# Conditioned hybrid layer on one core: the up-projection's half-size products for nine pairs of tiles in place of seven, and the MLP gate's first half computed earlier

## The chip, the core and the metric

The kernel runs on one core of a Trainium2 chip. Five engines work side by side, each through its own list of instructions: TensorE (PE, with its weight loads PEld), VectorE (DVE), ScalarE (ACT), GpSimd (POOL) and SyncE (SP), which here only issues DMAs. ACT and POOL issue DMAs too. They wait for one another on semaphores. The metric is the device time of one execution in microseconds, lower being better; all inputs and the output are fp32 in HBM.

## The reference

One decoder layer on 512 tokens with 1,024 channels: an attention part and a gated MLP, both conditioned by a vector c through `w_ada`. Only the second part and the end of the first matter here:

```python
mod = cs @ w_ada[l] + b_ada[l]
sh1, sc1, gt1, sh2, sc2, gt2 = [m[:, None, :] for m in jnp.split(mod, 6, axis=-1)]
...
mix = jnp.concatenate([o_hg, o_nsa], axis=-1) @ w_out[l]
x = x + gt1 * mix

h2 = rmsnorm(x, norm2_g[l]) * (1.0 + sc2) + sh2
u = causal_dwconv(h2 @ w_up[l], conv_w[l], conv_b[l])
a, v = jnp.split(u, 2, axis=-1)
x = x + gt2 * ((jax.nn.silu(a) * v) @ w_down[l])
```

`w_up` is 1024 x 5632 (two halves of D_FF = 2816, that is 22 tiles of 128 columns each), `w_down` 2816 x 1024. `gt2`, "the gate" in this document, is one row of 1,024 numbers, spread over all partitions.

## The kernel before

**Products.** Each fp32 operand is split into a rounded high part and the rest (`split`: ACT copies the high part, DVE subtracts), and each product is three matmuls (`mm3`, lines 156 to 158): high x high, high x low, low x high. All tiles of weights pass through this.

**Output projection** (lines 1577 to 1608 and the loop at 1948). Four token tiles i of 128 tokens. `hg_mix` normalises a tile's HGRN2 heads (an ACT square, a DVE sum, the power of `rstd` on POOL, a DVE multiply `on`), `hg_flip` transposes and splits it, `out_mm` multiplies, `out_sum` adds the residual and lets ACT sum the squares, `out_norm` turns them into the reciprocal root (DVE, then POOL's power), `out_scale` makes `hx`, and `h2_flip`, `h2_scale` and `h2_split` transpose it on TensorE, apply the conditioning and split it into `h2T`, the up-projection's right side. In the loop TensorE's list has `out_mm(i)` followed by `h2_flip(i - 1)`.

**Up-projection.** Stage st = 2f + s is tile f (0 to 21) of half s. A plain stage is `up_mm`: 8 blocks of 128 channels x 3 matmuls with 512 columns. `up_post` is the convolution (one ACT step, two DVE steps), then SiLU for s = 0 or the product with the other half for s = 1, after which `g_parts` lists the splits that the down-projection needs; the `x` tokens take them off the list one by one.

Tiles come in pairs: pair or unit j holds f = 2j and 2j + 1. In a unit, tile 2j (stages 4j and 4j + 1) is done by seven products P1 to P7 of half-size (Strassen's scheme over channel halves and token halves; `sprod`, four blocks x 3 matmuls with 256 columns), and tile 2j + 1 by two plain stages, called B and C. The product scheme needs sums of the weight quarters and of h2 (`hS`, eight granules of memory) and extra splits on ACT and DVE. The order within a unit is written out in `UNIT` (line 48); a token with a prime prepares the next unit. `PRO` (line 47) orders stages 0 to 7, `g` takes a step of the gate, `q` runs `up_post`. `NU = 8` is the last unit; the loop of line 1988 runs units 2 to 8, seven pairs. After it, the eight stages 36 to 43 run plain (lines 1993 to 2007, ordered by `PLAIN`, two of them with a low half made by a DMA that accumulates on POOL's queue).

**Memory.** `G` hands out one of 33 granules of 4 KB per partition. Each pair leaves two granules for the down-projection, `gP[j]` and `gQ[j]`, and parks others in HBM. `AWAY = (0, 1)` names the pairs whose `gQ` is parked too (`park`, DMA on ACT's queue) and read back in the first down phase (`load_away`, on SP's).

**The gate** (`ada_last`, line 1399). For each half of 512 columns: eight weight tiles from HBM, multiplied and added into an accumulator by DVE (lines 1410, 1415, 1420), a split, two matmuls with a matrix of ones (1426, 1427), an ACT copy. It is a generator: each `next(ada2)` does a step. The first half is stepped in `PRO` and in units 2 to 8, the second in the plain stages, all DMAs on SP's queue.

**Down-projection.** Again seven products, in three phases (`phase`) and a tail; `forms` prepares its weights, three forms ahead (`look`, `ready`), in buffers `whi`/`wlo` (two) and `aw` (one).

SP's, ACT's and POOL's DMA queues are worked off in program order, so a DMA that waits for its buffer holds up those behind it.

Of the kernel before, what the change touches and what calls it, by code (L numbers as in the profile page):

```python
# [20 lines left out]
P = 128  # L21
# [19 lines left out]
NB = 2  # L41
NU = 8
AWAY = (0, 1)
CUT = {"B": 6, "C": 7}
ADD = (1, 1)
PLAIN = "2 A1 1 1 A2 1 1 1"
PRO = ("t t g x M1 M2 t t t t F3 M3 F4 t A5 q0 M4 q1 q2 F6 q3 M5 M6 A7 x q4 g x q5 x t x n1' ns' f2' nc' n5' q6 na' g s4' m0' x x M7 m1' x f6' f7' x x x x f4'")
UNIT = ("P1 S P5 w n1' ns' x f3 B0 P6 P2 B1 V x f2' nc' n5' h1 x p-1 f4' P7 x m0' P3 h0' W p2 g p0 na' C0 P4 x x x C1 s4' p1 x m1' x f6' x x x f7'")
# [63 lines left out]
def hybrid_layer_kernel(ctx: ExitStack, tc: tile.TileContext, d: dict, out: bass.AP, dbg=None):  # L112
# [133 lines left out]

    made = [0]

    def form(src, added=False):

        made[0] += 1
        if made[0] % 3 != 2:
            hi = wp.tile(list(src.shape), F32R, tag="whi", name=nm("whi"))
            lo = wp.tile(list(src.shape), F32R, tag="wlo", name=nm("wlo"))
        else:
            t = wp.tile([P, 2] + list(src.shape)[1:], F32R, tag="aw", name=nm("w3"), bufs=1)
            hi, lo = t[:, 0], t[:, 1]
# [1019 lines left out]

    def hg_mix(i):
        ps = PS("hgo")
# [11 lines left out]
        r = SM([P, 8], "hrs")  # L1291
        rstd(r[:, 0:4], s[:, 0:4], 1.0 / P, 4.0 * EPS)
        on = TMP([P, 4, P], tag="on")
        ve.tensor_tensor(on, ps.rearrange("p (h e) -> p h e", h=4),
                         r[:, 0:4].unsqueeze(2).to_broadcast([P, 4, P]), ALU.mult)
        ons[i] = on

    def hg_flip(i):
        on = ons.pop(i)
        ps = PS()  # L1300
        for h in range(4):
            pe.transpose(ps[:, h * P:(h + 1) * P], on[:, h], ident)
        m = G([2, 4, P], F32R, s="mixH")
        t = TMP([P, 4, P], tag="og")
        for pr in range(2):
            ve.scalar_tensor_tensor(t[:, 2 * pr:2 * pr + 2], ps[:, pr * 256:pr * 256 + 256]
                                    .rearrange("p (h t) -> p h t", h=2), hgg,
                                    HGT[pr][:, :, i * P:(i + 1) * P], ALU.mult, ALU.mult)
        split(m[:, 0], m[:, 1], t)
        mixH[i] = m  # L1310
# [88 lines left out]
    def ada_last(s, res):  # L1399
        for q in range(2):  # L1400
            acc = res[:, q * 512:(q + 1) * 512]
            c0 = s * D + q * 512
            gp.memset(acc, 0.0)
            sp.dma_start(acc[0:1], d["b_ada"][:, c0:c0 + 512])
            for k in range(KT if q else 0):
                raw = TMP([P, 512], tag="ada2r")
                sp.dma_start(raw, ada_view[:, k, c0:c0 + 512])
                if k:
                    yield
                    ve.scalar_tensor_tensor(acc, last, cs[:, k - 1:k], acc, ALU.mult, ALU.add)  # L1410
                last = raw
            for k in range(0 if q else KT):
                last = res[:, 512:]
                if k:
                    ve.scalar_tensor_tensor(acc, last, cs[:, k - 1:k], acc, ALU.mult, ALU.add)
                sp.dma_start(last, ada_view[:, k, c0:c0 + 512])
                if k < KT - 1:
                    yield
            yield
# [6 lines left out]
            pe.matmul(ps, onesr, hi, start=True, stop=False)
# [150 lines left out]
    for i in range(NT):  # L1577
        x1.append(G([D], s="x1"))
        sp.dma_start(x1[i], x_view[:, i])
    next(gate1)  # L1580
    hg_mix(0)
    next(gate1)
    hg_mix(1)
    out_mm(0, 0, KN)
    cols_sum(acol)
    hg_flip(0)
    hg_mix(2)
    hg_mix(3)
    out_mm(1, 0, KN)
# [4 lines left out]
    hg_flip(1)  # L1594
    hg_flip(2)
    out_mm(3, 0, KN)
# [19 lines left out]
    def up_mm(st, sl, ks=range(KT)):  # L1616
        if st not in us:
            us[st] = PS("u")
            if st not in wts:
                wts[st] = next_parts(st < nst - 2, added=st >= 4 * NU + 4 and PLAIN.split()[st - 4 * NU - 4][0] == "A")  # L1620
        hi, lo = wts[st]
# [113 lines left out]
    def do(j, tok):  # L1735
        last = j == NU
        if tok.endswith("'"):
            if last:
                if tok in ("n1'", "m0'"):
                    piece()  # L1740
                return
            return do_(j + 1, tok[:-1])
        return do_(j, tok)

    def do_(j, tok):
        lo_, hi_ = lo_half, hi_half
# [71 lines left out]
    def g_parts(f, y):  # L1818
# [3 lines left out]
        if not odd:  # L1822
# [18 lines left out]
                     (split, st34[:, 0], st34[:, 1], s34),  # L1841
                     (lambda: None,),
                     (park, j, st22, st34)])

    def park(j, st22, st34):
        if j in AWAY:
            sc.dma_start(pk26[:, AWAY.index(j)], f32(gQ.pop(j)))
        sc.dma_start(pk22[:, j], f32(st22))
        sc.dma_start(pk34[:, j], f32(st34))
# [79 lines left out]

    def look():  # L1930
        w = next(source, False)
        if w is None:
            w = next(source)
        if w is not False:
            ready.append(w)

    def dn_out(acc, i, half, c0=0, c1=512):
# [5 lines left out]

    gt2 = wp.tile([P, D], F32, tag="xin", name="gt2", bufs=1)
    ada2 = ada_last(5, gt2)
    lo_half, hi_half, full = slice(0, 256), slice(256, 512), slice(0, 512)
    nst = 2 * NFF
    for i in range(NT):
# [24 lines left out]
    for tok in PRO.split():  # L1973
# [7 lines left out]
        elif tok[0] == "q":  # L1981
            up_post(int(tok[1]))
        elif tok[0] in "txg":
            do_(1, tok)
# [6 lines left out]
    assert not tw  # L1991
    first = 4 * NU + 4
    for st in range(first, nst):
        up_mm(st, full)
        if st >= nst - 2:
            look()
        if st == first:
            up_post(st - 1)
        elif st > first + 1:
            up_post(st - 2)  # L2000
        for _ in range(int(PLAIN.split()[st - first][-1])):
            next(ada2, None)

    look()
    up_post(nst - 2, False)
    bR, bW, bS, bV = ([PS("dn") for _ in range(2)] for _ in range(4))
# [101 lines left out]
```

## Time and profile before

| what | value |
|---|---|
| median of 3 runs (lowest to highest) | 675.23 us (674.49 to 675.26) |
| the profiled execution: its own time, its span | 674.35 us, 672.6 us |
| output projection's token loop | about 302 to 333 us |
| stages 0 to 7 | about 327 to 372 us |
| units 2 to 8 | 372.3 to 520.2 us |
| plain stages 36 to 43 | 520.2 to 563.8 us |
| down-projection | 564.2 us to the end |
| HBM traffic | 105.01 MB read, 13.90 MB written |

The span goes from the first to the last instruction of the program. In rows of the order of time, the first number is the start from the span's start, the second the duration, then engine, source line, operation, what is written and read, the shape, and in brackets the idle time of the engine before it and what ended it. Durations of matmuls overlap, so their price is read from the distance of their starts. A row of the waits gives the total, the number of waits and the longest.

### The profile page before, as it was taken

Reading aid. Unit: us, or ns where it says so; the run is one execution under the profiler, and the core shown is the slowest. Engines: PE = TensorE matmul, PEld = TensorE weight load, DVE = VectorE, ACT = ScalarE, POOL = GpSimd, SP = SyncE. Lnnn points to the kernel's source line nnn. Section 1 sums busy time; section 2 is a strip of 40 time slices with the busy share of each in tenths; the row PEclk is TensorE's granted clock in tenths of the full one; section 3 lists DMA queues with packets and bytes.
Section 4 is the critical chain, followed back from the end, with each engine's and each line's share of the span. In section 5 each row is a group of like instructions: output and inputs, shape, how many; then the busy total and the mean of one; then the engine's idle time right before and its main releaser. Section 6 shows DMA issues by size and latency. Waiting matters only on the chain.

```text
span 672.6 us, 10869 instructions
## 1 busy us (share of the span) xinstructions
PE 664.9 (99%) x3999; PEld 565.1 (84%) x3999; DVE 577.8 (86%) x1155; ACT 392.6 (58%) x757; POOL 60.0 (9%) x80
## 2 busy tenths in 40 slices
PE   8999999999999999999999999999999999999998
PEld 4678898788898889888998888989888888888886
DVE  5688988999998997687878988998898789988787
ACT  5564446666677688335665766667675455553431
POOL 1006144200000000200000011010110000000000
PEclk9999999999999999999999999999999999999999
DMA  9998444388042132435436677986779773979932
GB/s 279 287 322 269 145 157 138 106 288 254 11 147 95 33 107 99 172 96 161 140 95 172 179 196 198 242 218 175 187 181 277 217 234 124 393 259 398 388 112 94
DMA packets 110473, 128.52 MB, mean 191 GB/s; under 512 B 7067, under 2 KB 84691, under 8 KB 110421
## 3 DMA queue, kind: packets, MB, share of 16 engines
q1 hardware_dynamic: 103541, 106.89, 51.1%
q0 software_dynamic: 2448, 8.91, 6.9%
q10 hardware_dynamic: 4432, 12.04, 4.7%
q8 instruction: 31, 0.51, 0.3%
q14 instruction: 21, 0.17, 0.1%
HBM read 105.01 MB, written 13.90 MB: 177 GB/s over the span
## 4 chain that ended last, share of the span: by engine, by line
PE 92%; SPq 3%; DMA 2%; DVE 1%; issue 0%; ACTq 0%; ACT 0%
PE u L156 11%; PE u L158 11%; PE u L157 11%; PE dn L157 5%; PE dn L156 5%; PE dn L158 5%; PE pT L156 3%; PE pT L158 3%; PE pT L157 3%; PE F L1059 3%; PE oT L1087 3%; PE oh L158 2%; PE oh L156 2%; PE oh L157 2%; SPq L317 2%; PE lev L1188 2%
## 5 line engine op out<-in xcount | busy, mean ns | idle before, releaser
L156 PE MATMUL u<-h2h,whi 128*128 128x512 f32 (+1 forms) x208 | 78.0, 375 | 0.0
L157 PE MATMUL u<-h2l,whi 128*128 128x512 f32 (+1 forms) x208 | 77.8, 374 | 0.0
L158 PE MATMUL u<-h2h,wlo 128*128 128x512 f32 (+1 forms) x208 | 77.6, 373 | 0.0
L153 DVE TENSOR_TENSOR wlo<-raw,whi 128x1024 fp32r<-128x1024 f32 (+1 forms) x38 | 44.5, 1170 | 6.7 <-ACT whi L152 6.5
L152 ACT CAST whi<-raw 128x1024 fp32r<-128x1024 f32 (+1 forms) x38 | 38.3, 1008 | 18.8 <-PE u L157 7.3
L158 PEld LDWEIGHTS u<-h2h,wlo 128*128 128x128 f32 x208 | 39.2, 188 | 7.5 <-DVE wlo L153 0.4
L156 PEld LDWEIGHTS u<-h2h,whi 128*128 128x128 f32 x208 | 39.3, 189 | 6.0
L157 PEld LDWEIGHTS u<-h2l,whi 128*128 128x128 f32 x208 | 39.3, 189 | 5.8
L1027 ACT ACTIVATE pt<-pt,mx 128x128 f32<-128x128 f32 (+3 forms) x64 | 35.9, 562 | 11.8 <-DVE mx L1011 10.7
L1634 DVE SCALAR_TENSOR_TENSOR y<-u,cv,y 128x511 f32<-128x511 f32 x44 | 32.8, 745 | 11.4 <-ACT y L1633 11.4
L156 PE MATMUL pT<-hT,whi 128*128 128x512 f32 x96 | 39.2, 408 | 0.0
L1638 ACT ACTIVATE y<-y 128x512 f32<-128x512 f32 x21 | 13.3, 633 | 42.0 <-DVE y L1635 42.0
L158 PE MATMUL pT<-hT,wlo 128*128 128x512 f32 x96 | 37.7, 393 | 0.0
L157 PE MATMUL pT<-hT,whi 128*128 128x512 f32 x96 | 37.6, 391 | 0.0
L1011 DVE CUSTOM_DVE_ANT_0 pt<-S,cmask 128x128 f32<-128x128 f32 (+3 forms) x64 | 29.7, 484 | 6.5 <-PE S L1006 6.3
L1066 ACT COPY pT<-F 128x512 f32<-128x512 f32 (+2 forms) x52 | 25.9, 503 | 14.4 <-PE F L1059 11.2
L1635 DVE SCALAR_TENSOR_TENSOR y<-u,cv,y 128x510 f32<-128x510 f32 x44 | 32.9, 749 | 1.6
L1633 ACT ACTIVATE y<-u,cv 128x512 f32<-128x512 f32 x44 | 33.8, 771 | 0.0
L393 POOL TENSOR_TENSOR hrs<-hrs,mhalf 128x4 f32<-128x4 f32 (+2 forms) x16 | 20.0, 1259 | 136.4 <-DVE hrs L392 136.3
L157 PE MATMUL u<-h2l,w 128*128 128x256 f32 (+1 forms) x84 | 28.0, 333 | 0.0
L156 PE MATMUL u<-h2h,w 128*128 128x256 f32 (+1 forms) x84 | 28.0, 333 | 0.0
L158 PE MATMUL u<-h2h,w 128*128 128x256 f32 (+1 forms) x84 | 28.0, 333 | 0.0
(456 smaller groups left out, 2079.2 us busy)
## 6 DMA issues: line engine op xcount, KB each, us to landing
raw<-in_w_up SPq DMA_DIRECT2D x44, 512.0 KB, 5.6
aw<-in_w_ada SPq DMA_DIRECT2D x24, 512.0 KB, 3.6
raw<-in_w_down SPq DMA_DIRECT2D x10, 1024.0 KB
ada<-in_w_ada SPq DMA_DIRECT2D x32, 256.0 KB, 5.8
wlo<-raw POOLq DMA_DIRECT2D x15, 512.0 KB, 4.6
raw<-in_w_in SPq DMA_DIRECT2D x7, 1024.0 KB, 6.1
rawd<-in_w_down SPq DMA_DIRECT2D x12, 512.0 KB, 10.3
pk<-st ACTq DMA_DIRECT2D x11, 512.0 KB, 4.0
```

What stands on the lines that cost most here:

```text
L152: sc.copy(hi, src)
L153: (eng or ve).tensor_tensor(lo, src, f32(hi), ALU.subtract)
L156: pe.matmul(o, ah, bh, start=start, stop=False, skip_group_check=True)
L157: pe.matmul(o, ah, bl, start=False, stop=False, skip_group_check=True)
L158: pe.matmul(o, al, bh, start=False, stop=stop, skip_group_check=True)
L1011: ve.tensor_tensor_reduce(pt[:, sl], ps[:, sl], cmask[:, 512 - W:512], -1.0, 1e30, ALU.add, ALU.min, mx[:, e:e + 1])
L1027: sc.activation(pt[:, sl], pt[:, sl], AF.Exp, bias=mx[:, e:e + 1], scale=-1.0, accum_out=su[:, h % 2, e:e + 1])
L1059: pe.transpose(ps[:, j * P:(j + 1) * P], src[:, j * P:(j + 1) * P], ident)
L1066: sc.copy(pT, ps[:, 0:n * P])
L1633: sc.activation(y, u, AF.Identity, bias=cv[:, 132 + c:133 + c], scale=cv[:, 88 + c:89 + c])
L1634: ve.scalar_tensor_tensor(y[:, 1:], u[:, :T - 1], cv[:, 44 + c:45 + c], y[:, 1:], ALU.mult, ALU.add)
L1635: ve.scalar_tensor_tensor(y[:, 2:], u[:, :T - 2], cv[:, c:c + 1], y[:, 2:], ALU.mult, ALU.add)
```

## The change

`NU` becomes 10, so units 2 to 10, nine pairs, are done by half-size products and no stage after them is plain; `PLAIN` is empty and its loop is gone. `AWAY` grows to six pairs. In the last unit three tokens with a prime call `look` and so prepare the first three forms of the down-projection, the third of them in granules (`wide`). One more matmul of 256 columns stands behind the last unit's P1; it writes the half of its bank that P1 leaves out and that DVE overwrites later.

The gate's generator is cut into finer steps (40 in all, multiply and DMA apart). The first half runs during the output projection: its DMAs and bias go through POOL's queue, its multiplies stand between the steps of `hg_mix`, `hg_flip` and the token loop, and it is closed in `PRO` (split behind A5, matmuls ahead of stage 6, copy behind q5). The second half runs in `PRO`'s end and units 2 to 10, with its weights in a part of the constants that is no longer read, on SP's queue.

```diff
-NU = 8
-AWAY = (0, 1)
+NU = 10
+AWAY = (0, 1, 2, 3, 4, 5)
...
-PLAIN = "2 A1 1 1 A2 1 1 1"
-PRO = ("t t g x M1 M2 t t t t F3 M3 F4 t A5 q0 M4 q1 q2 F6 q3 M5 M6 A7 x q4 g x q5 x t x n1' ns' f2' nc' n5' q6 na' g s4' m0' x x M7 m1' x f6' f7' x x x x f4'")
+PLAIN = ""
+PRO = ("t t x M1 M2 t t t t F3 M3 F4 t A5 g q0 M4 q1 q2 F6 q3 M5 G M6 A7 x q4 x q5 G x t x n1' ns' f2' nc' n5' q6 na' s4' m0' x x M7 m1' g x f6' f7' x x x x f4'")
...
     def form(src, added=False):
-        made[0] += 1
-        if made[0] % 3 != 2:
+        made[0] += not wide[0]
+        if wide[0]:
+            hi, lo = (G(list(src.shape)[1:], F32R, s="wg") for _ in range(2))
+        elif made[0] % 3 != 2:
...
         rstd(r[:, 0:4], s[:, 0:4], 1.0 / P, 4.0 * EPS)
+        between()
         on = TMP([P, 4, P], tag="on")
...
-        split(m[:, 0], m[:, 1], t)
+        sc.copy(m[:, 0], t)
+        between()
+        ve.tensor_tensor(m[:, 1], t, f32(m[:, 0]), ALU.subtract)
...
     def ada_last(s, res):
         for q in range(2):
             acc = res[:, q * 512:(q + 1) * 512]
+            last = cb[:, C_LMASK:C_LMASK + 512] if q else res[:, 512:]
             c0 = s * D + q * 512
             gp.memset(acc, 0.0)
-            sp.dma_start(acc[0:1], d["b_ada"][:, c0:c0 + 512])
...
+            gp.dma_start(acc[0:1], d["b_ada"][:, c0:c0 + 512])
+            for k in range(KT):
                 if k:
                     ve.scalar_tensor_tensor(acc, last, cs[:, k - 1:k], acc, ALU.mult, ALU.add)
+                yield
+                (sp if q else gp).dma_start(last, ada_view[:, k, c0:c0 + 512])
+                yield
             ve.scalar_tensor_tensor(acc, last, cs[:, k:k + 1], acc, ALU.mult, ALU.add)
             hi = TMP([P, 512], F32R, tag="rhi")
             lo = TMP([P, 512], F32R, tag="rlo")
             split(hi, lo, acc)
             yield
+            yield
             ps = PS()
             pe.matmul(ps, onesr, hi, start=True, stop=False)
             pe.matmul(ps, onesr, lo, start=False, stop=True)
+            yield
             sc.copy(acc, ps)
             yield
+
+    def gate_step(n=2):
+        for _ in range(n):
+            next(ada2, None)
...
+    gt2 = wp.tile([P, D], F32, tag="xin", name="gt2", bufs=1)
+    ada2 = ada_last(5, gt2)
+    gate_step()
     next(gate1)
     hg_mix(0)
     next(gate1)
-    hg_mix(1)
+    hg_mix(1, partial(gate_step, 1))
+    gate_step(1)
     out_mm(0, 0, KN)
...
-    hg_mix(3)
+    hg_mix(3, partial(gate_step, 1))
+    gate_step(1)
...
-    hg_flip(2)
+    hg_flip(2, partial(gate_step, 1))
+    gate_step(1)
...
             if last:
-                if tok in ("n1'", "m0'"):
-                    piece()
+                if tok in ("nc'", "m0'", "na'"):
+                    look(tok == "na'")
                 return
...
             sprod(u(1, lo_), w[1], h2_quarter(0, lo_), True)
+            if last:
+                pe.matmul(u(1, hi_), w[1][0][:, 0], h2_quarter(0, lo_)[0][0], start=False, stop=False,
+                          skip_group_check=True)
...
-        elif tok == "g":
-            next(ada2, None)
+        elif tok in ("g", "G"):
+            gate_step(2 if tok == "g" else 1)
...
-                     (lambda: None,),
+                     (park_q, j),
                      (park, j, st22, st34)])
...
-    def park(j, st22, st34):
+    def park_q(j):
         if j in AWAY:
             sc.dma_start(pk26[:, AWAY.index(j)], f32(gQ.pop(j)))
...
         sc.dma_start(x1d[:, i], x1[i])
+        gate_step(1)
         out_norm(i)
+        gate_step(1)
...
-    first = 4 * NU + 4
-    for st in range(first, nst):
-        up_mm(st, full)
...
-    look()
-    up_post(nst - 2, False)
+    gate_step()
+    assert next(ada2, 0) == 0
...
         if k == 0:
-            sc.activation(ys[nst - 2], ys[nst - 2], AF.Silu)
+            pass
         elif k == 1:
             up_post(nst - 1)
         elif k % 2:
             step(3)
-            load_away(k // 2 - 1)
+            load_away(k - 3)
+            load_away(k - 2)
```

More of the change, by code (lines that the diff above doesn't have):

```diff
@@ L247, in hybrid_layer_kernel @@
     made = [0]
+    wide = [False]
     def form(src, added=False):
-        made[0] += 1
-        if made[0] % 3 != 2:
+        made[0] += not wide[0]
+        if wide[0]:
+            hi, lo = (G(list(src.shape)[1:], F32R, s="wg") for _ in range(2))
+        elif made[0] % 3 != 2:
             hi = wp.tile(list(src.shape), F32R, tag="whi", name=nm("whi"))
@@ L1276, in hybrid_layer_kernel, with hg_mix @@
     mixH = [None] * NT
-    def hg_mix(i):
+    def hg_mix(i, between=lambda: None):
         ps = PS("hgo")
@@ L1296, in hg_mix, with hg_flip @@
         ons[i] = on
-    def hg_flip(i):
+    def hg_flip(i, between=lambda: None):
         on = ons.pop(i)
@@ L1401, in ada_last @@
             acc = res[:, q * 512:(q + 1) * 512]
+            last = cb[:, C_LMASK:C_LMASK + 512] if q else res[:, 512:]
             c0 = s * D + q * 512
             gp.memset(acc, 0.0)
-            sp.dma_start(acc[0:1], d["b_ada"][:, c0:c0 + 512])
[L1405 to L1413, printed above, removed]
+            gp.dma_start(acc[0:1], d["b_ada"][:, c0:c0 + 512])
+            for k in range(KT):
                 if k:
                     ve.scalar_tensor_tensor(acc, last, cs[:, k - 1:k], acc, ALU.mult, ALU.add)
[L1416 to L1419, printed above, removed]
+                yield
+                (sp if q else gp).dma_start(last, ada_view[:, k, c0:c0 + 512])
+                yield
             ve.scalar_tensor_tensor(acc, last, cs[:, k:k + 1], acc, ALU.mult, ALU.add)
@@ L1619, in up_mm @@
             if st not in wts:
-                wts[st] = next_parts(st < nst - 2, added=st >= 4 * NU + 4 and PLAIN.split()[st - 4 * NU - 4][0] == "A")
+                wts[st] = next_parts(st < nst - 2, added=False)
         hi, lo = wts[st]
@@ L1745, in do_ @@
     def do_(j, tok):
+        last = j == NU
         lo_, hi_ = lo_half, hi_half
@@ L1841, in g_parts, with park @@
                      (split, st34[:, 0], st34[:, 1], s34),
-                     (lambda: None,),
+                     (park_q, j),
                      (park, j, st22, st34)])
-    def park(j, st22, st34):
+    def park_q(j):
         if j in AWAY:
             sc.dma_start(pk26[:, AWAY.index(j)], f32(gQ.pop(j)))
+    def park(j, st22, st34):
         sc.dma_start(pk22[:, j], f32(st22))
@@ L1928, in sums_first, with look @@
             raise AssertionError
-    def look():
+    def look(g=False):
+        wide[0] = g
         w = next(source, False)
@@ L1935, in look @@
             ready.append(w)
+        wide[0] = False
     def dn_out(acc, i, half, c0=0, c1=512):
@@ L1942, in dn_out @@
         sp.dma_start(out_view[:, i, cols], t)
-    gt2 = wp.tile([P, D], F32, tag="xin", name="gt2", bufs=1)
-    ada2 = ada_last(5, gt2)
     lo_half, hi_half, full = slice(0, 256), slice(256, 512), slice(0, 512)
@@ L1982, in hybrid_layer_kernel @@
             up_post(int(tok[1]))
-        elif tok[0] in "txg":
+        elif tok[0] in "txgG":
             do_(1, tok)
@@ L1991, in hybrid_layer_kernel @@
     assert not tw
-    first = 4 * NU + 4
-    for st in range(first, nst):
-        up_mm(st, full)
-        if st >= nst - 2:
-            look()
[L1997 to L2006, printed above, removed]
-    up_post(nst - 2, False)
+    gate_step()
+    assert next(ada2, 0) == 0
     bR, bW, bS, bV = ([PS("dn") for _ in range(2)] for _ in range(4))
```

## The prediction

> **What bounds the kernel now.** I read the page first, then the waits of the weight loads, then TensorE's order of time for the last pairs of tiles, then the same stretches for the other engines.
>
> ```profile
> span 672.6 us, 10869 instructions
> PE 664.9 (99%) x3999; PEld 565.1 (84%) x3999; DVE 577.8 (86%) x1155; ACT 392.6 (58%) x757; POOL 60.0 (9%) x80
> PE 92%; SPq 3%; DMA 2%; DVE 1%; issue 0%; ACTq 0%; ACT 0%
> PEld u L158 <- DVE wlo L153: 0.4, 1, 0.4
> PEld dn L157 <- DVE wlo L153: 0.3, 1, 0.3
> ```
>
> TensorE is 92% of the chain that ended last. The two PEld rows are all that weight loads waited for another engine from 300 us on. So every matmul issued less is time won, as long as the others keep pace; and whatever another engine delays beyond its slack is lost whole. The price of a product is the distance between starts, since durations overlap:
>
> ```profile
> 477.72 0.28 PE L156 MATMUL u<-h2h,w 128*128 128x256 f32 x1
> 477.84 0.28 PE L157 MATMUL u<-h2l,w 128*128 128x256 f32 x1
> ...
> 498.75 0.28 PE L156 MATMUL u<-h2h,w 128*128 128x256 f32 x1
> ...
> 520.23 0.40 PE L156 MATMUL u<-h2h,w 128*128 128x512 f32 x1
> ...
> 563.76 0.39 PE L1426 MATMUL ps<-rhi,onesr 128*128 128x512 f32 x1
> ...
> 564.21 0.39 PE L156 MATMUL dn<-whi,gP 128*128 128x512 f32 x1
> ```
>
> Half-size matmuls (256 columns) start 0.12 us apart. Unit 7 runs from 477.72 to 498.75, **21.03 us**. The eight plain stages run from 520.23 to 563.76, **43.53 us**, 5.44 each or 0.227 for each of 24 full matmuls (512 columns). Half a gate costs two matmuls, 0.45 us (563.76 to 564.21).
>
> **The change part by part.** *TensorE's sum.* The eight plain stages go and units 9 and 10 come, each seven half-size products and two full stages: 2 x 21.03 = 42.06. That is **-1.47 us**. The columns saved are those of six full matmuls a unit, which would be 1.4 us; but 84 half-size matmuls at 0.12 are 10.1 us, where the 48 full ones that they replace are 10.9, so a unit wins 0.8 or less. The extra matmul after P1 of the last unit has 256 columns: **+0.12**. The four gate matmuls change places only: the first half's go from unit 8 to a place ahead of stage 6, the second half's into unit 10. **0.**
>
> *Do units 9 and 10 hold unit 7's pace?* Unit 7 already carried what unit 9 will: the preparation of the next unit, the gate's last multiply and its split.
>
> ```profile
> 477.72:498.75 21.03, 21.03 (x134) 19.08 (x133) 18.93 (x35) 14.87 (x26) 1.75 (x2) 1.00 0.79 200
> 520.23:563.76 43.53, 43.53 (x194) 36.04 (x193) 36.41 (x58) 22.19 (x36) 1.75 (x2) 1.00 0.65 207
> 393.60:414.60 21.00, 21.00 (x133) 19.07 (x132) 18.60 (x35) 14.19 (x25) 1.73 (x2) 1.00 0.83 222
> 399.84 0.33 ACTq L1847 DMA_DIRECT2D pk<-gQ  x1
> ```
>
> The columns are PE, PEld, DVE, ACT, POOL, then clock and DMA share. DVE is busy 18.93 of 21.03 us, so about 2 us of each unit are left to it: tight, but TensorE leads. The four new parks (512 KB each, in units 3 to 6) are covered by unit 3, which parks one granule today (399.84) at a DMA share of 0.83 and shows 21.00 busy of 21.00. If that cover failed, ACT would be late by 0.33 us of issue a unit, of its 6 us of idle time. **0.**
>
> In the last unit the first three down weights replace the next unit's preparation:
>
> ```profile
> L153 DVE TENSOR_TENSOR wq<-raw,wq 128x512 fp32r<-128x512 f32 x35 | 23.9, 685 | 0.7 <-ACT wq L152 0.7
> 554.75 1.22 DVE L153 TENSOR_TENSOR wlo<-raw,whi 128x1024 fp32r<-128x1024 f32 x1
> 576.19 1.22 DVE L153 TENSOR_TENSOR wlo<-keep,whi 128x1024 fp32r<-128x1024 f32 x1
> ...
> 577.81 0.39 PE L156 MATMUL dn<-whi,gP 128*128 128x512 f32 x1
> ```
>
> Ten 512-column operations of 0.69 (6.9 us) leave DVE, five of 1,024 columns at 1.22 (two sums and three low halves, 6.1 us) come. The tightest form of the first down phase is ready at 577.41 (576.19 + 1.22), 0.4 us before its product at 577.81. Afterwards the third form is made before stage 43's matmuls, not after them, and stage 42's convolution too, so DVE enters the phase with less behind it. Bounds: 0.4 better than now to 0.4 of stall; I take **0**, from the DVE sum.
>
> *The first half of the gate moves* from units 2 to 8 into the output projection: seven multiplies on DVE, eight weight loads and the bias from SP's queue to POOL's. In the loop over the four token tiles each multiply stands where DVE waits today:
>
> ```profile
> 310.93 0.55 POOL L393 TENSOR_TENSOR rs<-rs,mhalf 128x1 f32<-128x1 f32 x1 [24.84 <-DVE rs L392]
> 311.51 0.89 DVE L1522 TENSOR_SCALAR hx<-x,rs 128x512 f32<-128x512 f32 x2 [0.66 <-POOL rs L393]
> 314.30 0.69 DVE L1510 TENSOR_TENSOR x<-x,tmp 128x512 f32<-128x512 f32 x1
> 315.78 0.16 DVE L1515 TENSOR_TENSOR ss<-ss 128x1 f32<-128x1 f32 x1 [0.79 <-ACT sq L1512]
> ...
> 331.33 0.87 DVE L1522 TENSOR_SCALAR hx<-x,rs 128x512 f32<-128x512 f32 x2
> ...
> 332.70 0.49 PE L1532 MATMUL ps<-cb,hx 128*128 128x128 f32 x3
> 332.86 0.87 PE ps L1532 x8
> ...
> 373.28 0.75 DVE L1415 SCALAR_TENSOR_TENSOR gt<-gt,cs 128x512 f32<-128x512 f32 x1
> 373.94 0.69 DVE L1685 TENSOR_TENSOR raw<-raw 128x512 f32<-128x512 f32 x1
> ```
>
> A multiply of 0.75 fits the gap of 0.79 (314.99 to 315.78), if its weights have landed. Its DMA is issued on POOL behind the rstd power, at 311.48 (310.93 + 0.55); the next multiply wants it at 314.99, **3.5 us** later. No row has this DMA; the nearest are these:
>
> ```profile
> gt<-in_w_ada SPq DMA_DIRECT2D x8, 256.0 KB, 2.8
> wlo<-raw POOLq DMA_DIRECT2D x15, 512.0 KB, 4.6
> rawd<-in_w_down SPq DMA_DIRECT2D x12, 512.0 KB, 10.3
> 502.48 0.87 POOL L1695 DMA_DIRECT2D wlo<-raw  x1 [9.16 <-ACT gP L152]
> DMA  9600000019910010000279799999950000796006
> ```
>
> The same bytes land in 2.8 us from SP; POOL's issue takes 0.87 of work, so I take 3.3 (nearest: same bytes, same source, half a microsecond for POOL). Ends: 2.8 and 10.3, the latter from a stage with full DMA engines. The last row is the DMA share from 311 to 333 us, 0.55 us a digit: the engines stand idle from 312 to 315, when the first of these transfers flies. Behind a waiting multiply on DVE stand ss, rstd, the scaling of h2 and of hx, the low halves and the next weight's subtraction; TensorE waits for hx. At the last transposes hx is complete at 332.20 (331.33 + 0.87), and its second half is wanted four transposes of 0.11 (0.87 for eight) after the start at 332.70: **0.9 us of slack**. At the taken 3.3 us the term is **0**; at 10.3 it is the slow rival below. The three multiplies before the loop stand in DVE's waits for POOL's power or for an ACT copy, and their weights were issued a whole step earlier: 0, and at worst the 0.1 by which a multiply overhangs its gap.
>
> *Stages 4 to 7.* The one stall, unit 2's first B matmul:
>
> ```profile
> 345.86 1.22 DVE L153 TENSOR_TENSOR hS<-hB,hS 128x1024 fp32r<-128x1024 f32 x1
> 347.20 0.77 ACT L1633 ACTIVATE y<-u,cv 128x512 f32<-128x512 f32 x1
> 374.55 1.22 DVE L153 TENSOR_TENSOR wlo<-raw,whi 128x1024 fp32r<-128x1024 f32 x1
> 375.42 0.40 PE L157 MATMUL u<-h2l,whi 128*128 128x512 f32 x1
> 375.82 0.50 PE L158 MATMUL u<-h2h,wlo 128*128 128x512 f32 x1
> ```
>
> The step there takes 0.40 where 0.23 is usual, and the next is long too: I put the loss at 0.26. The change takes the multiply at 373.28 away (-0.66, to the start of the next at 373.94) and puts a multiply, an ACT copy and a subtraction ahead of the first convolution. The multiply can start when DVE is through at 347.0 (345.86 + 1.22, overlapping a little) and ends at 347.7, the copy of 0.6 ends at 348.3, so the ACT step now at 347.20 slips by about 1.05. DVE then reaches this weight 0.39 late, while the two gate matmuls ahead of stage 6 move TensorE itself 0.45 on. The stall goes from 0.26 to about 0.2: **-0.08** at most, which I take. Ends: -0.26 (gone) and +0.4 (the slip counts whole). This is an estimate from these rows.
>
> **Sum:** -1.47 + 0.12 - 0.08 = **-1.43 us**. The profiled execution took 674.35 us, 1.75 around its span of 672.6; the median of the runs shown, 675.23, lies 0.88 above it. So the profiled execution would be 672.9 and the median **673.8 us**, or -0.21%. About 0.2% (1.35 us) is what a measurement of this kernel can tell from no change: the forecast sits on that line.
>
> **The rivals.** *Given back (chance 0.18):* the slip ahead of stage 4, or the entry to the down phase, costs 0.3 to 1.2 us, the term left at 0 there. For it: slack of 0.4 at 577.81 and DVE's chain in front of 374.55. Against: the DVE sum is lighter in the last unit. Time 674.1 to 675.0.
>
> *Slower (0.12):* the gate's DMAs on POOL land late in the token loop. With a landing of L, DVE is late by L - 3.5 in the second turn and by about L - 5.2 more in each of the next two (those turns are 7 us apart, 6.45 of wait and 0.54 of work on POOL, where the second follows the first by 5.3); TensorE loses that less 0.9. At L = 5.4 this is 1.4 and eats the gain; at 6.5 it is 4.7, time 678.5. Against it: the idle DMA engines in the row above and the 4.6 of twice the bytes; for it: 10.3 under load.
>
> ```profile
> 323.21 0.54 POOL L393 TENSOR_TENSOR rs<-rs,mhalf 128x1 f32<-128x1 f32 x1 [6.45 <-DVE rs L392]
> ```
>
> One mechanism would push it there without load: hx is scaled (0.89 for two, 0.45 each, where x's addition of as many elements takes 0.69) just where POOL issues the DMA; if POOL has to wait for it, L grows by up to 0.9. I give that case 0.04 of the 0.12. The Trainium skill ("SBUF — State Buffer", SBUF: two separate sides) says that DVE in its two-port mode locks POOL out and so holds up descriptors of DMAs from POOL's queue. No row here shows it. By that rule, and with the 4.6 of twice the bytes, L would be 5.5: DVE 2.6 late, TensorE 1.7, time 675.5.
>
> *It does not do what it says (0.04):* reloading six granules adds 2 MB in the first down phase, where
>
> ```profile
> 563.80:594.00 30.20, 30.20 (x135) 25.02 (x134) 27.72 (x37) 17.84 (x26) 0.00 (x0) 1.00 0.84 326
> ```
>
> DMA share is already 0.84 at 326 GB/s; 2.1 MB more at that rate is 6.4 us of backlog. If the next weights wait for it, TensorE loses 1 to 3 us: 675 to 677. Against it: the reloaded granules are wanted one phase later, from about 594 on.
>
> **How the numbers follow.** Forecast 0.66, split 0.42 faster to 0.24 same, since its own range is 673.2 to 674.4 around a line at 673.9. Given back 0.18, all same. Slower rival 0.12: 0.10 slower, 0.02 same. The last 0.04: half and half. Faster 0.42, same 0.46, slower 0.12. Range: down to 672.6 (the waits of both PEld rows gone, -1.35 - 0.26 - 0.3 = -1.9, and 0.7 for the runs' own spread, 674.49 to 675.23), up to 675.8 (1.2 given back, 675.0, and as much spread); the slow rival beyond it is left out.
>
> **What would show it.** Right: P1 of units 9 and 10 21.0 us apart, the last unit 21.6 with gate and extra matmul, the first dn matmul near 562.8, no DVE wait on a gate DMA in the token loop, no PEld wait beyond those two. Wrong: a TensorE wait on hx's transposes, on wlo ahead of unit 2, or on dn in the first products.

## The result: slower by 7 us, and the profile after

| | time, us | ratio to the kernel before, with its 95% interval |
|---|---|---|
| kernel before, 5 runs beside it | 675.23 (674.32 to 675.29) | |
| changed kernel, 5 runs | 682.31 (681.23 to 683.38) | 1.011 [1.0096, 1.0124] |
| forecast | 673.8 (672.6 to 675.8) | 0.998 |

The profiled execution of the changed kernel took 681.23 us around a span of 679.5. The page of the changed kernel, its first lines and the chain of work that ended last:

```profile
span 679.5 us, 11071 instructions
PE 666.9 (98%) x4072; PEld 567.0 (83%) x4072; DVE 586.2 (86%) x1175; ACT 399.7 (59%) x773; POOL 68.3 (10%) x92
PE 64%; DVE 17%; DMA 6%; ACT 5%; SPq 4%; issue 2%; ACTq 1%; DVEq 0%
```

TensorE's share of the chain fell from 92% to 64%, while its busy share of the span fell by one point only. A busy share does not show who sets the end. The waits of the weight loads from 300 us on do (total, number, longest), in the changed kernel:

```profile
PEld u L156 <- ACT u L1781: 6.3, 6, 1.3
PEld dn L157 <- DVE wlo L153: 3.0, 3, 1.8
PEld u L158 <- DVE wlo L153: 1.0, 1, 1.0
```

Before there were two such rows, of 0.4 and 0.3 us. The new first row is product P6, which waits six times for ACT's copy of token S (line 1781 now). The changed kernel by unit, from the view by stretches (same columns as in the prediction):

```profile
372.36:394.75 22.39, 21.62 (x133) 18.95 (x132) 19.42 (x34) 15.09 (x26) 2.80 (x4) 1.00 0.77 209
...
438.49:460.69 22.20, 21.30 (x134) 19.00 (x133) 19.40 (x35) 14.30 (x25) 1.72 (x2) 1.00 0.81 214
...
504.74:525.76 21.02, 21.02 (x133) 19.07 (x132) 19.17 (x35) 14.29 (x25) 1.75 (x2) 1.00 0.79 202
...
546.79:568.16 21.37, 21.37 (x135) 19.38 (x134) 17.71 (x30) 12.62 (x22) 0.88 (x1) 1.00 0.64 209
```

Units 2 to 7, the six in which a `gQ` is parked, take 21.8 to 22.4 us. Units 8 and 9 take 21.02 and 21.03, as forecast. The last window ends one matmul ahead of the down phase; to the phase's first product at 568.39 (below) the last unit takes 21.60, as forecast too. In TensorE's order of time:

```profile
424.34 0.38 PE L156 MATMUL u<-hS,wq 128*128 128x256 f32 x1 [0.68 <-ACT u L1781]
...
568.39 0.40 PE L156 MATMUL dn<-w,gP 128*128 128x512 f32 x1
...
576.56 0.39 PE L156 MATMUL dn<-whi,gP 128*128 128x512 f32 x1
578.34 0.50 PE L157 MATMUL dn<-wlo,gP 128*128 128x512 f32 x1 [1.39 <-DVE wlo L153]
```

The first product of the down phase starts at 568.39 and not near 562.8; from 372.36 to there are 196.0 us, where the forecast's own terms make 189.8 (nine units of 21.03, a gate half of 0.45, the extra matmul): **6.2 us** are lost in units 2 to 7. In the first down phase two more stalls, at the fourth and the sixth form, take **1.9** of PE's time; the phase and what follows are 2.7 us longer than before (111.1 from 568.39 to the end, 108.4 before from 564.21). In these two profiles the output projection and its token loop lost nothing: unit 2 starts at 372.36, where it started at 372.32.

### The profile page after: what moved, and what is told of

It reads as the page before. It is cut to its first block, busy times and chain, and to the rows that moved or that the text cites. A ratio compares the mean times of both kernels' runs of the same rounds, so it can differ in the third digit from the quotient of the medians.

```text
span 679.5 us, 11071 instructions
## 1 busy us (share of the span) xinstructions
PE 666.9 (98%) x4072; PEld 567.0 (83%) x4072; DVE 586.2 (86%) x1175; ACT 399.7 (59%) x773; POOL 68.3 (10%) x92
## 3 DMA queue, kind: packets, MB, share of 16 engines
q0 software_dynamic: 3440, 12.06, 8.6%
q10 hardware_dynamic: 5008, 14.13, 5.4%
## 4 chain that ended last, share of the span: by engine, by line
PE 64%; DVE 17%; DMA 6%; ACT 5%; SPq 4%; issue 2%; ACTq 1%; DVEq 0%
PE dn L157 5%; PE dn L158 4%; PE dn L156 4%; PE u L156 3%; DMA raw<-in_w_up 3%; PE u L157 3%; PE u L158 3%; PE pT L156 3%; PE pT L158 3%; PE pT L157 3%; DVE y L1645 3%; DVE y L1644 3%; PE F L1062 3%; PE oT L1090 3%; SPq L320 2%
## 5 line engine op out<-in xcount | busy, mean ns | idle before, releaser
L158 PE MATMUL u<-h2h,wlo 128*128 128x512 f32 (+1 forms) x200 | 74.5, 373 | 0.5 <-DVE wlo L153 0.5
L156 PE MATMUL u<-h2h,whi 128*128 128x512 f32 (+1 forms) x200 | 75.0, 375 | 0.0
L157 PE MATMUL u<-h2l,whi 128*128 128x512 f32 (+1 forms) x200 | 74.8, 374 | 0.0
L158 PEld LDWEIGHTS u<-h2h,wlo 128*128 128x128 f32 x200 | 37.7, 188 | 7.7 <-DVE wlo L153 1.0
L156 PEld LDWEIGHTS u<-h2h,whi 128*128 128x128 f32 x200 | 37.8, 189 | 5.5
L153 DVE TENSOR_TENSOR wlo<-raw,whi 128x1024 fp32r<-128x1024 f32 (+1 forms) x31 | 35.9, 1159 | 3.5 <-ACT whi L152 3.4
L1648 ACT ACTIVATE y<-y 128x512 f32<-128x512 f32 x22 | 13.9, 633 | 40.5 <-DVE y L1645 40.5
L152 ACT CAST whi<-raw 128x1024 fp32r<-128x1024 f32 (+1 forms) x31 | 30.9, 998 | 10.0 <-PE kva L158 4.4
L152 ACT CAST wq<-raw 128x512 fp32r<-128x512 f32 x45 | 27.7, 617 | 14.7 <-DVE gQ L153 10.4
L156 PE MATMUL u<-hS,wq 128*128 128x256 f32 x108 | 31.0, 287 | 3.8 <-ACT u L1781 3.8
L153 DVE TENSOR_TENSOR wq<-raw,wq 128x512 fp32r<-128x512 f32 x45 | 30.8, 686 | 3.1 <-ACT wq L152 3.1
```

The lines of the kernel that those rows point to most:

```text
L153: (eng or ve).tensor_tensor(lo, src, f32(hi), ALU.subtract)
L156: pe.matmul(o, ah, bh, start=start, stop=False, skip_group_check=True)
L157: pe.matmul(o, ah, bl, start=False, stop=False, skip_group_check=True)
L158: pe.matmul(o, al, bh, start=False, stop=stop, skip_group_check=True)
```

## The experiments

All twelve change a few lines of one of the two kernels. "Over" is the median less that of the kernel before in the same set of runs; for the changed kernel itself it is 7.08.

| run | over, us | ratio [95%] |
|---|---|---|
| 1 parks back behind S | 6.70 | 1.0093 [1.0078, 1.0108] |
| 2 before, its two parks early | 1.12 | 1.0015 [1.0006, 1.0025] |
| 3 splits after the forms | 7.39 | 1.0108 [1.0093, 1.0123] |
| 4 runs 1 and 3 together | 6.40 | 1.0089 [1.0074, 1.0105] |
| 5 parks on POOL's queue | 9.33 | 1.0135 [1.0118, 1.0152] |
| 6 before, six parks | 4.38 | 1.0063 [1.0048, 1.0078] |
| 7 run 5, SiLUs later | 7.86 | 1.0111 [1.0096, 1.0126] |
| 8 SiLUs later | 5.80 | 1.0084 [1.0069, 1.0099] |
| 9 parks in the idle stretch | 2.05 | 1.0027 [1.0015, 1.0039] |
| 10 parks of 8 KB | 1.75 | 1.0029 [1.0019, 1.0038] |
| 11 runs 9 and 8 together | -0.16 | 0.9997 [0.9988, 1.0006] |
| 12 run 11, gate's end after stage 0 | -0.95 | 0.9986 [0.9977, 0.9995] |

### First theory: the place of the parks in ACT's queue

The waits point at ACT. Its order of time around one S copy of the changed kernel (an ACTq row is the issue of a DMA):

```profile
423.03 0.33 ACTq L1861 DMA_DIRECT2D pk<-gQ  x1
423.39 0.62 ACT L152 CAST wq<-raw 128x512 fp32r<-128x512 f32 x1 [1.91 <-DVE gQ L153]
423.49 0.37 ACTq L1864 DMA_DIRECT2D pk<-st  x1
423.92 0.37 ACT L1781 COPY u<-u 128x256 f32<-128x256 f32 x1
423.96 1.12 ACTq L1865 DMA_DIRECT2D pk<-st  x1
```

The change moved the park of `gQ` one list step ahead, from behind token S to in front of it. There it waits for DVE's split of `gQ`, and the S copy stands behind it. Runs 1 and 2 move this one step, in either kernel:

```diff
-                     (park_q, j),
+                     (lambda: None,),
                      (park, j, st22, st34)])
...
     def park(j, st22, st34):
+        if j in AWAY:
+            sc.dma_start(pk26[:, AWAY.index(j)], f32(gQ.pop(j)))
```

Run 1:

> The changed kernel, with the six parks of gQ put back into the step that follows token S, beside the two other parks; bytes and number of parks are the same. Theory A (ACT's queue): the park issued one step earlier makes ACT wait for DVE's split of gQ in front of the S copy, and P6 waits for that copy. Then units 3 to 7 take 21.0 us each instead of 21.8 to 22.2, unit 2 at most 21.6, the S copy starts 5.1 to 6.3 us after its unit instead of 7.2 to 7.8, and the time falls by 5.5 to 6.2 us, to about 676.4. Rival B (traffic): it is the 2 MB more of parks in a stretch with DMA busy at 0.8 that hold up the weights. Then units 2 to 7 stay at 21.7 to 22.4 us and the time at 682 within 1 us.

Run 2, the reverse edit in the kernel before:

> The kernel before, with only its two parks of gQ moved one step ahead, in front of token S, as in the changed kernel. Bytes are the same. Theory A: units 2 and 3 gain a stall at P6 of 0.6 to 1.2 us each, the other units stay at 21.03; the time rises by 1.2 to 2.2 us to about 676.9. Rival B: nothing changes, 675.2 within 0.7.

Run 1 took 681.52 us: units 3 and 4 came down to 21.03 and 21.17, but units 5 to 8 then took 22.1 to 22.4. From the view by stretches of run 1:

```profile
394.88:415.91 21.03, 21.03 (x133) 19.07 (x132) 18.26 (x34) 14.20 (x25) 1.71 (x2) 1.00 0.80 219
...
459.14:481.56 22.42, 21.72 (x134) 18.89 (x132) 19.21 (x35) 14.48 (x27) 1.76 (x2) 1.00 0.80 211
```

So the place is not the main cause. It is a cost where there are few parks: run 2 took 675.94 beside 674.82, with units 2 and 3 at 22.11 and 21.37 and the next at 21.03. In the changed kernel its share (7.08 less 6.70) is too small for the two intervals to tell.

### The down phase, first attempt

The fourth form was late, and DVE does four splits from the list of `x` steps just ahead of it. Run 3 leaves the five list steps behind C1 of the last unit to the first down phase:

```diff
+        if tok == "C1":
+            closed[0] = last
+        if tok == "x" and closed[0]:
+            return
...
         elif k % 2:
-            step(3)
+            step(5)
```

> The changed kernel, with the five list steps (splits for the down-projection) that follow C1 in the last unit left to the first down phase, which then takes five steps at a time instead of three. Units as in the changed kernel. Theory C (DVE's order at the entry): the fourth form of the first down phase is late because 1.9 us of DVE's splits stand ahead of it. Then it is ready 1.6 us sooner, the stall of 1.7 us at its product falls to at most 0.2, and the time falls by 1.0 to 2.2 us, to about 680.6. Rival D (the reloads): the first down phase is late because 2 MB more come in through SP's queue. Then the stalls in it stay at 2.4 us together, and the time at 682 within 0.7.

Run 4 is run 3 with the parks as in run 1:

> Both edits in the changed kernel: parks of gQ behind token S, five list steps of the last unit left to the first down phase. Theories A and C: the sum of both, 7.0 to 8.2 us less than the changed kernel, 674.2 to 675.3, which is the kernel before or up to 1 us better. Rivals B and D: above 681.

Run 3 took 682.21, run 4 681.22; run 3's waits of weight loads in the down phase:

```profile
PEld dn L157 <- DVE wlo L153: 3.1, 5, 1.3
...
PEld dn L157 <- DVE w L153: 0.6, 1, 0.6
```

The stall at the fourth form went and came back at the sixth and later ones. Order alone does not help: DVE is late as a whole.

### Second theory: ACT's issues; and the parks alone

Run 1 left a third DMA issue in a row on ACT (1.12 us in the row above, where the first takes 0.33). If that is what delays ACT, the parks of `gQ` must go to another queue. Run 5:

```diff
     def park_q(j):
         if j in AWAY:
-            sc.dma_start(pk26[:, AWAY.index(j)], f32(gQ.pop(j)))
+            gp.dma_start(pk26[:, AWAY.index(j)], f32(gQ.pop(j)))
```

> The changed kernel, with the six parks of gQ issued on POOL's queue at the place of the change, instead of on ACT's; same bytes at the same moment, and ACT neither waits for DVE's split of gQ nor issues a third DMA in a unit. Theory A2 (ACT's queue): moving the parks behind S did not help beyond two units because a third DMA issue in a row keeps ACT's queue for 1.1 us longer, and ACT, DVE and the weights' loads hand on to one another with less than that to spare in a unit, so the lag grows from unit to unit. Then all units from 3 on take 21.03 us, and the time falls by 5 to 6 us to about 676.5. Rival B (traffic): the bytes themselves hold up the weights. Then units 2 to 7 stay between 21.6 and 22.2 us and the time above 681.

Run 6, in the kernel before:

```diff
-AWAY = (0, 1)
+AWAY = (0, 1, 2, 3, 4, 5)
...
-            load_away(k // 2 - 1)
+            load_away(k - 3)
+            load_away(k - 2)
```

> The kernel before, with six pairs' gQ parked instead of two (on ACT, behind token S, as there) and read back two a step in the first down phase; gate, units and plain stages as before. Theory A2 and rival B both: units 4 to 7 slow down one after the other as in the changed kernel with the parks put back, by up to 1 us each, so 2 to 4 us in all, about 678. Rival E (the other parts of the change, the gate's second half in the units and its loads, take the slack): units stay at 21.03 and the time at 675 within 0.7.

Run 5 took 683.89, no less than the changed kernel. Units 4 to 8 take 22.0 to 22.7 us, although ACT is free of these parks and each of its two other issues in a unit takes only 0.33 us: the theory falls. From its view by stretches (unit 5) and, below, its waits:

```profile
438.00:460.70 22.70, 21.72 (x134) 18.96 (x132) 19.02 (x36) 14.34 (x26) 2.29 (x3) 1.00 0.78 208
```

```profile
PEld u L156 <- ACT u L1781: 4.7, 6, 1.0
PEld u L158 <- DMA wlo<-raw: 3.3, 4, 1.3
```

The second row is not among those of the changed kernel (run 1 has it with 0.8 us in two waits): matmuls wait for a low half that a DMA makes on POOL's queue. It is not the park that holds up POOL's next issue, which waits another 8.6 to 10.2 us for ACT. The Trainium skill ("DMA: Bandwidth & Descriptors", Issuing engines are not separate DMA queues) says that DMAs from any issuing engine run on the same 16 DMA engines, and another issuer saves only the sequencer's time. Run 5 agrees: another issuer, no gain. Why it was worse than run 1 by 2.6 us stays open; the longer waits for POOL's DMAs are one difference.

Run 6 shows the rest. Six parks alone cost the kernel before 4.38 us, and its units slow down one by one; units 3 to 7 in its view by stretches:

```profile
393.34:414.37 21.03, 21.03 (x134) 19.08 (x133) 18.52 (x34) 14.20 (x25) 1.73 (x2) 1.00 0.84 224
414.37:435.39 21.02, 21.02 (x133) 19.07 (x132) 18.13 (x34) 14.20 (x25) 1.75 (x2) 1.00 0.82 221
435.39:456.64 21.25, 21.25 (x133) 19.01 (x132) 18.77 (x34) 13.41 (x24) 1.75 (x2) 1.00 0.80 214
456.64:478.82 22.18, 21.63 (x133) 18.90 (x132) 18.33 (x35) 13.67 (x25) 1.76 (x2) 1.00 0.81 215
478.82:501.64 22.82, 21.84 (x133) 18.89 (x132) 19.58 (x36) 14.70 (x26) 1.75 (x2) 1.00 0.79 207
```

The second and the third parking unit look as if a park cost nothing; the fourth loses 0.2 us, the fifth 1.2, the sixth 1.8. A lag builds up that the first units can still absorb: ACT's S copy starts 4.95, 5.47, 6.43, 7.37 and 8.00 us after the start of these five units. Unit 8 parks no `gQ` and still takes 22.88, where it took 21.48.

### Third theory: bytes inside a burst

The same view of the kernel before: 3.0 us near the start of unit 5, the 13.5 us behind them, and the whole unit:

```profile
437.20:440.20 3.00, 3.00 (x21) 2.70 (x20) 2.93 (x6) 3.00 (x7) 0.88 (x1) 1.00 0.01 3
441.70:455.20 13.50, 13.50 (x86) 12.21 (x86) 11.63 (x21) 8.45 (x13) 0.87 (x1) 1.00 1.02 273
435.67:456.69 21.02, 21.02 (x133) 19.07 (x132) 18.96 (x35) 14.29 (x25) 1.75 (x2) 1.00 0.82 208
```

The mean DMA share of that unit, 0.82, is made of nothing for 3 us and full engines for 13.5. The reason is in the waits of SP's queue, kernel before, 390 to 520 us:

```profile
SPq L223 <- DVE wq L153: 96.1, 6, 17.1
```

Once a unit SP stands for some 16 us at the next weight load, until DVE has read the old weights. Then all loads go out at once. ACT waits for them (four times in this stretch, 8.0 us together), DVE works on what ACT splits, and DVE's reading of these releases the next ones: a loop. Half a MB of park is in flight just when the full stretch starts: the `gQ` park of unit 3 is issued 6.2 us into its unit (399.84), and the burst above starts 6.0 us into unit 5. From the page of the changed kernel, queue, packets, MB and share of 16 engines:

```profile
q1 hardware_dynamic: 102961, 106.89, 50.2%
q0 software_dynamic: 3440, 12.06, 8.6%
q10 hardware_dynamic: 5008, 14.13, 5.4%
```

By its MB, q10 is ACT's queue with the parks: 5.4% of 679.5 us for 14.13 MB, 2.6 us a MB, so by this estimate a park of 0.52 MB takes all engines for about 1.4 us. Two runs test this. Run 9 parks later, where the engines idle; run 10 keeps every park and its waits and takes away the bytes, so the values of the six `gQ` are left out of its output.

Run 9:

```diff
-                     (split, st22[:, 0], st22[:, 1], y[:, h2]),
+                     (park_split, j, st22[:, 0], st22[:, 1], y[:, h2]),
...
-                     (park_q, j),
+                     (lambda: None,),
...
+    def park_split(j, *a):
+        park_q(j - 1)
+        split(*a)
```

> The changed kernel, with each gQ park issued about 16 us later, on ACT ahead of the split st22 of the next pair: number, bytes and queue of the parks as in the change. Theory B2 (the burst): in a unit the DMA engines stand idle for some 3 us near its start and are full for some 14 us after it, because the loads wait for their buffers; half a MB more inside that burst, 1.7 us at 310 GB/s, delays the weights by more than the 0.8 us or so that a unit can spare, and the lag carries over. A park in the idle stretch costs nothing. Then units 3 to 10 take 21.03 us (the last 21.6), and the time falls by 5 to 6 us to about 676.8. Rival F (a park costs by itself, by its issue, its wait or the granule that it holds): units 3 to 7 stay above 21.5 us and the time above 680.

Run 10, on run 1:

```diff
-            sc.dma_start(pk26[:, AWAY.index(j)], f32(gQ.pop(j)))
+            sc.dma_start(pk26[:, AWAY.index(j), 0, 0, 0:16], f32(gQ.pop(j))[:, 0, 0, 0:16])
...
-            sp.dma_start(f32(gQ[AWAY[n]]), pk26[:, n])
+            sp.dma_start(f32(gQ[AWAY[n]]), pk34[:, AWAY[n]])
```

> The changed kernel with the parks behind token S, as in the first experiment, and each gQ park cut to 16 columns (8 KB instead of 512); in the first down phase other parked data of the same size are read back, so the values of six pairs' gQ are left out. Every DMA, wait and granule stays. Theory B2: without the bytes, units 3 to 10 take 21.03 us and the time falls to 676 within 0.7. Rivals A2 and F: units 5 to 8 stay at 22.1 to 22.4 us and the time at 681.5.

Run 9 took 676.79 and run 10 676.49, as the third theory had it. Beside run 1, run 10 differs by the parks' bytes (the reads back keep their size): **5.0 us**. ACT's third issue in a row is down to 0.33 us in it as well, but so are ACT's issues in run 5, which won nothing. Beside the changed kernel, run 9 differs by when the same bytes are written, and with it by the park's place in ACT's list, for which run 1 shows 0.4 us, within the noise: 5.0 us too. It holds each `gQ` some 15 us longer in memory, so a later release of its granule is not what costs. Unit 4 of run 9, then 3.0 and 13.9 us of it:

```profile
416.73:437.76 21.03, 21.03 (x134) 19.07 (x133) 18.86 (x35) 14.29 (x26) 1.75 (x2) 1.00 0.82 223
...
417.90:420.90 3.00, 3.00 (x22) 2.78 (x21) 2.93 (x5) 3.00 (x7) 0.88 (x1) 1.00 0.31 124
422.80:436.70 13.90, 13.90 (x90) 12.64 (x88) 11.87 (x21) 8.17 (x12) 0.87 (x1) 1.00 0.93 256
```

The share of the whole unit (0.82) is no lower than in the stalled unit of the changed kernel (0.81); the idle stretch went from 0.01 to 0.31 and the burst is no longer full. All units from 3 to 9 take 21.02 or 21.03 us.

### The down phase, second attempt

DVE at the end of the last unit, changed kernel, order of time:

```profile
565.12 0.75 DVE L1645 SCALAR_TENSOR_TENSOR y<-u,cv,y 128x510 f32<-128x510 f32 x1
567.78 0.75 DVE L1644 SCALAR_TENSOR_TENSOR y<-u,cv,y 128x511 f32<-128x511 f32 x1 [1.91 <-ACT y L1643]
```

And ACT at the same place:

```profile
565.96 0.63 ACT L1648 ACTIVATE y<-y 128x512 f32<-128x512 f32 x1 [5.29 <-DVE y L1645]
566.49 0.57 ACT L1428 COPY gt<-ps 128x512 f32<-128x512 f32 x1
566.96 0.78 ACT L1643 ACTIVATE y<-u,cv 128x512 f32<-128x512 f32 x1
```

ACT is held at a SiLU until DVE ends a convolution at 565.87; the ACT step that DVE needs next is queued behind the SiLU and the gate's copy. DVE, which has the work to make the forms, stands for 1.91 us. Run 8 puts the SiLUs behind both ACT steps, in the last unit only:

```diff
         elif tok[0] == "p":
-            up_post(4 * j + int(tok[1:]))
+            up_post(4 * j + int(tok[1:]), not (last and tok in ("p2", "p0")))
+            if last and tok == "p0":
+                for st in (4 * j + 2, 4 * j):
+                    sc.activation(ys[st], ys[st], AF.Silu)
```

> The changed kernel, with one edit at the end of the last unit: the SiLU of stage B stands behind the ACT step of the next convolution instead of in front of it. Leaving five splits for later only moved the stall from the fourth form to the sixth, so DVE's work as a whole is late. Theory C2: it is late because DVE stands idle for 1.9 us ahead of that convolution, whose ACT step is queued behind a SiLU that waits for DVE itself. Then that idle time goes, the forms are ready about 1.9 us sooner, the two stalls (1.9 us in the first down phase) go down to 0.4 or less, and the time falls by 1.5 to 2.2 us to about 680.3. Rival D (the lag that DVE brings from the units): the idle time moves elsewhere and the stalls stay above 1.2 us.

Run 7 is this edit on run 5:

> The changed kernel with both edits: gQ parks on POOL's queue, and in the last unit the SiLUs of its plain stage B and of its first stage behind both convolutions' ACT steps. Theories A2 and C2: 7 to 8.4 us less than the changed kernel, 673.9 to 675.2. Rivals: above 680 (B) or 2 us more (C2 wrong).

Run 8 took 680.36. The same DVE step in it, now without idle time in front, and below it the down phase's waits of weight loads:

```profile
565.84 0.74 DVE L1644 SCALAR_TENSOR_TENSOR y<-u,cv,y 128x511 f32<-128x511 f32 x1
```

```profile
PEld dn L157 <- DVE wlo L153: 0.9, 2, 0.6
```

With the idle time 2.1 of the 3.0 us of waits are gone. Six reloads still come in during this phase, so they were not what held it. From the first down product to the end run 8 takes 109.1 us, still 0.7 more than the kernel before; what makes up this rest stays open.

The kernel before has the same wait at the end of its own last unit, where no next unit is prepared either:

```profile
517.35 0.75 DVE L1634 SCALAR_TENSOR_TENSOR y<-u,cv,y 128x511 f32<-128x511 f32 x1 [1.92 <-ACT y L1633]
```

Plain stages followed there, and TensorE lost nothing by it: that unit takes 21.48 us, 21.03 and half a gate. In units 2 to 9 of the changed kernel DVE's waits for this ACT step are 0.77 us at most. Run 7 (682.42) lost what run 5 loses: 1.5 us better than that, and far from its expectation of 674 to 675, which had rested on the second theory.

Run 11 joins the two edits that held:

> Both edits in the changed kernel: gQ parks in the idle stretch, and SiLUs of the last unit behind the convolutions' ACT steps. Theory B2 and C2: 7 to 8 us less than the changed kernel, 674.0 to 675.3 beside about 674.8 for the kernel before: what the change was worth by TensorE's sum, less what unit 2 loses at its first products. Rival F: above 679.

It took 674.58, even with the kernel before. The sum of TensorE's matmuls was worth about 1.4, so something was still lost, and it lay at the start of unit 2.

### The gate's end ahead of stage 0

DVE in the changed kernel, between the last h2 sum and the first convolution, and at unit 2's first B weight:

```profile
346.58 0.74 DVE L1418 SCALAR_TENSOR_TENSOR gt<-gt,cs 128x512 f32<-128x512 f32 x1
348.00 0.69 DVE L153 TENSOR_TENSOR rlo<-gt,rhi 128x512 fp32r<-128x512 f32 x1 [0.69 <-ACT rhi L152]
348.68 0.75 DVE L1644 SCALAR_TENSOR_TENSOR y<-u,cv,y 128x511 f32<-128x511 f32 x1
...
375.15 1.23 DVE L153 TENSOR_TENSOR wlo<-raw,whi 128x1024 fp32r<-128x1024 f32 x1 [0.37 <-ACT whi L152]
```

Run 12 moves one token of `PRO` in run 11:

```diff
-F4 t A5 g q0 M4
+F4 t A5 q0 g M4
```

> The kernel of the run before (parks in the idle stretch, SiLUs later) with one token of PRO moved: the gate's last multiply and its split stand behind the convolution of stage 0 instead of ahead of it. Theory G (the slip counts whole): the multiply, the ACT copy and the wait between them put off the first convolution by 1.2 us, and everything behind it, to the low half for unit 2's first B product, which loses 0.87 us; behind the convolution DVE stands idle for 2.7 us anyway. Then unit 2 takes 21.0 to 21.3 us instead of 21.9, and the time falls by 0.6 to 0.9 us to about 673.8, that is 1 us or 0.15% below the kernel before. Rival H (the loads into unit 2, or ACT's other steps, hold it): unit 2 stays at 21.8 us and the time at 674.6.

It took **673.64 us**, 0.14% below the kernel before (interval 0.05 to 0.23%), the fastest version of this study. Its waits of weight loads, and two of its units (view by stretches):

```profile
PEld dn L157 <- DVE wlo L153: 0.9, 2, 0.6
PEld u L158 <- DVE wlo L153: 0.4, 1, 0.4
```

```profile
373.09:394.40 21.31, 21.31 (x134) 19.00 (x133) 19.08 (x34) 15.14 (x27) 2.80 (x4) 1.00 0.77 197
...
541.58:563.18 21.60, 21.60 (x136) 19.57 (x135) 19.52 (x32) 13.71 (x24) 0.88 (x1) 1.00 0.64 207
```

Unit 2 went from 21.9 to 21.31; the last unit, with gate half and extra matmul, takes the 21.6 that the prediction named.

## Why the prediction was wrong, step by step

- **TensorE's sum (-1.47, +0.12): right.** In run 12 TensorE goes from unit 2's start (373.09) to the down phase (563.18) in 190.1 us, where the kernel before took 191.9; 0.45 of this is the gate half that now lies ahead of unit 2. Over the whole kernel -0.95 is left of the -1.35.
- **"The four new parks ... are covered by unit 3": the step that failed, by 5.0 us.** Three readings were wrong. The new parks do not lie in units 3 to 6 but in units 4 to 7: unit 3 holds the second of the two old ones, so it could speak for two parks in a row and not for six. It showed 21.00 of 21.00 because the first units can take in a park's delay, not because parks are free; run 6 needs the fourth parking unit to show the first 0.2 us, and the sixth loses 1.8. And "if that cover failed, ACT would be late by 0.33 us of issue a unit, of its 6 us of idle time" priced the instruction and not its bytes: run 5 took the instruction off ACT and won nothing, run 10 kept it and took away the bytes, and units 3 to 9 are back at 21.02 to 21.03. The DMA share of 0.83 that was read as room is a mean over an idle stretch and a full one.
- The park's **place** was not weighed at all: the step was moved ahead of token S, and nothing named the S copy as queued behind its wait. Run 2 prices this at 1.1 us for two parks; among six it can't be told apart.
- **Units 9 and 10 hold the pace: right** (21.03, and 21.60 for the last one in the changed kernel; half a gate and the extra matmul are in it).
- **"I take 0, from the DVE sum" at the entry to the down phase: wrong**, outside its own bounds of 0.4. The operations were counted rightly (ten out, five in); what the sum left out is the wait between two engines, 1.91 us on DVE, which the profile before showed too (1.92 at 517.35). Without the next unit's preparation there was no work left to fill it. Run 8 wins 1.3 us over the changed kernel, run 11 wins 2.2 over run 9. The rival "given back" named this place and the next one, at 0.3 to 1.2 us in all; they cost 2.2 and 0.8.
- **Stages 4 to 7 (-0.08, ends -0.26 and +0.4): wrong, past its upper end.** In run 11, where nothing else holds unit 2, the stall that was 0.26 is 0.87 (unit 2 takes 21.90 us). The slip ahead of stage 4 was of the forecast size (1.05): in the changed kernel the first convolution's ACT step starts at 347.88, 3.20 us after stage 3's first matmul (344.68), before at 347.20, 2.11 after it (345.09). But the multiply removed at 373.28 (0.66) did not give all of its time back: in front of the low half DVE now waits 0.37 us for ACT's high half, which starts 1.73 us into unit 2 where it started 1.07 into it. Run 12 is 0.8 us better than run 11.
- **The slower rival, the gate's loads in the token loop: refuted.** They landed in 3.1 us (3.3 taken), and DVE's only waits from 300 to 334 us are those for POOL's power and for TensorE. From the changed kernel's DMA issues (KB each, median us to landing) and its waits:

```profile
gt<-in_w_ada POOLq DMA_DIRECT2D x8, 256.0 KB, 3.1
```

```profile
DVE hx L1526 <- POOL rs L396: 0.7, 1, 0.7
DVE hB L1549 <- PE ps L1536: 0.2, 1, 0.2
```

  The delay of POOL's descriptors that the Trainium skill ("SBUF — State Buffer", SBUF: two separate sides) would allow does not show in these rows; they cannot say whether DVE ran in such a mode there.
- **It does not do what it says (reloads): refuted** by run 8, in which the reloads stay and most of the stalls go, and by run 6, which has the six reloads and takes 108.3 us from the first down product to the end, as before (108.4). The rival on the slower side that did come, parks' bytes inside the burst of loads, was not among those named.

## What to carry to other kernels

A stage that shows no stall once does not show that it can repeat: look whether the followers (here the S copy, 4.95 to 8.00 us into its unit in run 6) start later from round to round, since slack that is being used up looks like slack that is there. Read the DMA share in pieces of a few microseconds before calling a transfer covered; where loads wait for buffers, as here, a store belongs into the stretch in which the loads can't run yet. And an engine's sum of work is a lower bound: an in-order queue that hands work to and fro with another needs its waits counted too, above all where the filling work of the next round is missing.

## What the hardware showed unexpectedly

- DMAs of different kinds take the engines for different times a byte. By the page rows above, the queue with POOL's DMAs, most of which accumulate into a low half, takes 8.6% of 679.5 us for 12.06 MB, 4.8 us a MB; SP's loads take 3.2 and ACT's parks 2.6. By that, the two accumulating loads of 0.52 MB in a unit take all engines for an estimated 5.0 us, a park for 1.4. The queues' packets differ in size too (3.5, 1.0 and 2.8 KB on average), so the rows do not show how much of this is due to the kind.
- Issues in a row can get slower: of ACT's three DMAs above the first takes 0.33 us, the third (as many bytes) 1.12. It is 1.08 to 1.12 in units 3 to 7 of the changed kernel, though 0.47 in unit 2; in unit 8, where two DMAs start 1.9 us apart, each takes 0.33. As run 5 shows, that was not what the time was lost to.
